# Fetching gathered rows and modulation weights ahead of their use, and keeping the first gates of a dense expert layer on chip

## The chip, the cores and the metric

The kernel runs on one core of a Trainium2 chip. TensorE (PE; its weight loads are PEld) multiplies matrices, VectorE (DVE) and ScalarE (ACT) do elementwise work, GpSimd (POOL) does some more of it and issues DMAs of its own, SyncE (SP) issues the other DMAs. Each engine takes its instructions strictly in order, and semaphores join them. The metric is the device time of one launch in microseconds (us). A measurement of this kernel can tell about 0.2% from no change.

## The reference, cut to what matters

Two networks run after one another on 256 tokens of 1024 columns in f32: a first block of two layers (gated feed-forward, then retention or latent attention with a memory, then feed-forward again), and a second block of two layers in which every norm is modulated by a vector computed from a conditioning input, and the feed-forward is a mixture of 16384 tiny experts:

```python
ml = (silu(c) @ mod_w[i] + mod_b[i]).reshape(bsz, 1, 6, d)      # modulation rows, latent
mc = (silu(c_ctx) @ mod_w[i] + mod_b[i]).reshape(6, d)          # the same for the context
xl = rmsnorm(hl, norm1_g[i]) * (1.0 + ml[:, :, 1]) + ml[:, :, 0]
...
def _peer_ffn(x, w_q, keys, u, v):       # 8 heads, 16 experts a head and token, of 128 x 128
    ...
    a = jnp.einsum('nd,nhkd->nhk', xt, u[eidx])
    w = gate * gelu(a)
    return jnp.einsum('nhk,nhkd->nd', w, v[eidx])
```

The second block has 256 context tokens beside the 256 latent ones. They pass through its first layer only.

## The kernel before

**Two streams.** The program is written by two generators that `run_streams` takes in turn. The main stream does the first block, then the even mixer, the expert layer `peer_dense(x, 0, 0)`, the odd mixer, `peer_dense(x, 1, 0)` and the final norm. The side stream does what the second block needs beforehand: modulation rows, the context's even mixer, its routing, and its expert layer. Each stream has a clock; what a generator yields is added to it (on the side divided by `s.rate`), the stream that is behind goes on, and the clock becomes the priority by which a scheduler orders the instructions of each engine. So a yielded number decides where an instruction stands. While a side ring of weight tiles is open, `dq` issues the side's DMAs on POOL, and otherwise on SP.

**Modulation.** Twelve slots of 1024 outputs, six a layer. A slot reads 4 MB of `modw` in eight tiles of 512 KB (`raw`, line 197, from a ring of `RN` = 3 tiles), and TensorE multiplies each tile in eight short matmuls (line 877). Two slots are done at the start, three beside the context's even mixer, the other seven (`mod1`) along with the gather. 96 tiles in all, each fetched where its matmuls are recorded.

**Context experts (gather).** For each of two tiles of 128 tokens, 128 rows of `u` are gathered by indirect DMA (`pg`, line 1586), one row a token at a time, and multiplied with the tokens by a DVE dot (line 306); then 128 rows of `v` are gathered and added up (line 1604). 512 gathers in all, into a ring of `GR` = 6 tiles. The odd mixer waits for the last of it (`hc1`).

**Latent experts (peer_dense).** All 16384 experts are multiplied densely, as 64 pairs of 256. `up` multiplies the tokens with `u` of a pair and keeps the result in `A`; `down` multiplies `A` with the gates of the pair (line 1686), splits the product into a high part `Wh` and a low part `Wl` (lines 259, 260), splits the weights of `v` likewise (`wh`, `wl`, lines 248, 255) and does three matmuls for each product (`mm3`, lines 357 to 359). Between the two, `spread_gates` turns the routing into dense gates in 16 blocks of 16 tokens: three DVE operations (`OJ`, `OI`, `OM`), 32 matmuls (line 1637), copies into a stage `Gst`, and a DMA of each block to DRAM (`Gd`). `down` reads them back by four pairs (`Gq`). `A0N` ups come before the spread, one a block follows until `AR` tiles of `A` are full, and the rest alternate with `down`. The first `NU` ups are single f32 products (line 404), the others are split into three.

Of the kernel before, what the change touches and what calls it, by code (L numbers as in the profile page):

```python
# [19 lines left out]
D = 1024  # L20
# [146 lines left out]
class Kern:  # L167
# [681 lines left out]
            yield from s.out_proj(x, mix, d["wo1"], g3)  # L849


    def modulation(s, l, side, slots):


        nc, d = s.nc, s.d
        qs = [(slice(32 * j, 32 * j + 32), slice(256 * j, 256 * j + 256)) for j in range(4)]
        with s.pool("mod", side) as pl:
            c = pl.tile([128, 8, 32], F32, name=s.nm("cT"))
            nc.vector.memset(c, 0.0)
            cr = pl.tile([128, 8, 2], F32, name=s.nm("cR"))  # L860
            s.dq(cr, d["cvecT"])
            nc.scalar.activation(c[:, :, 0:2], cr, AF.Silu)
            one = pl.tile([128, 32], F32, name=s.nm("one"))
            nc.vector.memset(one, 1.0)
            for a in slots:
                dr = s.dramp.tile([2, D], F32, name=s.nm("modd"))
                bias = pl.tile([128, 256], F32, name=s.nm("modb"), tag="modb")
                s.dq(bias[0:128:32], d[f"modb{l}"][0, a * D:(a + 1) * D].rearrange("(j n) -> j n", j=4))
                if a in (1, 4):
                    g = pl.tile([128, 256], F32, name=s.nm("modg"), tag="modg")  # L870
                    s.dq(g[0:128:32], d["n12r"][2 * l + a // 4].rearrange("(j n) -> j n", j=4))
                pb = s.bank("c")
                for k0 in range(0, 8, 2):
                    raw = s.load(d[f"modw{l}"][:, (a * 8 + k0) * D:(a * 8 + k0 + 2) * D])
                    for k in range(2):
                        for ps, ns in qs:
                            nc.tensor.matmul(pb[ps, :256], c[:, k0 + k], raw(k * D + ns.start, k * D + ns.stop),  # L877
                                             start=(k0 + k == 0), stop=False)
                    yield 3.0
                for ps, ns in qs:  # L880
                    nc.tensor.matmul(pb[ps, :256], one[ps.start:ps.start + 1], bias[ps.start:ps.start + 1], start=False, stop=True)
                o = pl.tile([128, 256], F32, name=s.nm("modo"), tag="modo")
                if a in (1, 4):
                    pg = s.bank("c")
                    for ps, ns in qs:
                        nc.tensor.matmul(pg[ps, :256], one[ps.start:ps.start + 1], g[ps.start:ps.start + 1], start=True, stop=True)
                    nc.vector.tensor_scalar(o, pb[:, :256], 1.0, None, op0=OP.add)
                    nc.vector.tensor_tensor(o, o, pg[:, :256], op=OP.mult)
                else:
                    nc.vector.tensor_copy(o, pb[:, :256])  # L890
                for v in range(2):
                    s.dq(dr[v].rearrange("(j n) -> j n", j=4), o[v:128:32])
                    s.mod[l, v, a] = dr[v:v + 1]
# [330 lines left out]
    def even(s, ep, x, l, v, C, kind, tk, side):  # L1224
# [4 lines left out]
        with s.pool("evo", side) as po:  # L1229
# [41 lines left out]
            with s.pool("eva", side) as pl:  # L1271
                if lat:
                    ks = ("acc", "w", "c")
                    yield from s.mlstm(pl, E, C, R, mix, ks)
                    yield from s.diff_attn(pl, E, C, R, mix, ks)
                else:
                    yield from s.taking_turns(s.mlstm_ctx(pl, E, R, mix, "c"), s.diff_attn_ctx(pl, E, R, mix, "c"),
                                              s.modulation(0, side, [2, 4, 3]))
            with s.pool("evp", side) as pl:
                xT = s.xt_tiles(None if lat else pl)  # L1280
                g = s.modrow(l, v, 2, pool=pl, tag="gate")
# [296 lines left out]
    def gather(s, hc, l, v, side, also):  # L1578

        nc, d = s.nc, s.d  # L1580
        xmd, eidx, gates = s.picks
        with s.pool("pgg", side) as op:
            for t in range(2):
                def gath(tab, k):
                    gt = op.tile([128, D], F32, tag="pgt", name=s.nm("pg"), bufs=s.gring)
                    nc.gpsimd.indirect_dma_start(out=gt, out_offset=None, in_=d[tab],  # L1586
                                                 in_offset=bass.IndirectOffsetOnAxis(ap=eidx[t][:, k:k + 1], axis=0))
                    return gt
                xm = op.tile([128, D], F32, tag="pxy", name=s.nm("pxm"))
                s.dq(xm, xmd[t])  # L1590
                A = op.tile([128, 128], F32, tag="pA", name=s.nm("pA"))
                for k in range(128):
                    s.pin(s.dot(gath("u0", k), xm, A[:, k:k + 1]))
                    if k % 2:
                        yield s.gcost + s.along(also)
                nc.scalar.activation(A, A, AF.Gelu)
                nc.vector.tensor_tensor(A, A, gates[t], op=OP.mult)
                y = op.tile([128, D], F32, tag="pxy", name=s.nm("py"))
                for k in range(128):
                    gt, wk = gath("v0", k), A[:, k:k + 1]  # L1600
                    if k == 0:
                        s.pin(nc.vector.tensor_scalar(y, gt, wk, None, op0=OP.mult))
                    else:
                        s.pin(nc.vector.scalar_tensor_tensor(y, gt, wk, y, op0=OP.mult, op1=OP.add))  # L1604
                    if k % 2:
                        yield s.gcost + s.along(also)
                g = s.modrow(l, v, 5, pool=op, tag="pgt", bufs=s.gring)
                x = op.tile([128, D], F32, tag="pgt", name=s.nm("px"), bufs=s.gring)
                s.dq(x, hc[t])
                nc.vector.tensor_tensor(y, y, g, op=OP.mult)  # L1610
                nc.vector.tensor_tensor(x, x, y, op=OP.add)
                s.dq(s.hc1[t], x)
                yield 0


    def spread_gates(s, Gd, IJ, gg, io, step):


        nc = s.nc
# [1 line left out]
        for b in range(256 // TB):  # L1621
# [11 lines left out]
            for t0 in range(0, TB, 4):  # L1633
                pb = s.bank("c")
                for t in range(4):
                    for k in range(2):
                        nc.tensor.matmul(pb[:, t * 128:(t + 1) * 128], M[:, k, :, t0 + t], OJ[:, (t0 + t) // 2, :, t % 2],  # L1637
                                         start=(k == 0), stop=(k == 1))
                nc.scalar.activation(st[:, :, t0:t0 + 4], pb.rearrange("p (t j) -> p j t", t=4), AF.Copy, scale=2.0 ** -15)
            s.dq(Gd[b], st.rearrange("p j t -> p (j t)"))  # L1640
            yield from step()

    def peer_dense(s, x, l, v):
        nc, d = s.nc, s.d
        TB = 16
        NP = 64
        A0N, AR = ((8, 21), (18, 36))[l]
        NU = (AR, A0N)[l]
        ud, vd = d[f"ut{l}"], d[f"v{l}"].rearrange("(i j) n -> i j n", j=128)
        with s.pool("pd") as op:  # L1650
# [18 lines left out]
                As[q] = op.tile([128, 2, 256], F32, tag="A", name=s.nm("A"), bufs=AR)  # L1669
                nc.scalar.activation(As[q].rearrange("p a b -> p (a b)"), pb, AF.Gelu)  # L1670

            Gq = {}

            def gates(q):

                if q < NP:
                    Gq[q] = sp.tile([128, 16, 8, TB], F32, tag="Gq", name=s.nm("Gq"), bufs=2)
                    s.dq(Gq[q].rearrange("p b j t -> p b (j t)"),
                         Gd[:, :, q * 2 * TB:(q + 4) * 2 * TB].rearrange("b p n -> p b n"))

            def down(q):
                raw = s.load(vd[:, 2 * q:2 * q + 2])
                w = As.pop(q)
                g = Gq[q // 4 * 4][:, :, q % 4 * 2:q % 4 * 2 + 2].rearrange("p b j t -> p j b t")
                wv = w.rearrange("p j (b t) -> p j b t", b=16)
                nc.vector.tensor_tensor(wv, wv, g, op=OP.mult)
                wh = sp.tile([128, 2, 256], F32R, tag="Wh", name=s.nm("Wh"), bufs=2)
# [31 lines left out]
            with s.pool("psp") as s.spp:  # L1719
                s.share = SH[l][1]  # L1720

                def step():
                    if nup[0] < AR:
                        up()
                        yield 5.2
                yield from s.spread_gates(Gd, IJ, gg, io, step)
            xfp.__exit__(None, None, None)
            with s.pool("ps") as sp:
                s.share = SH[l][2]
                gates(0)  # L1730
                for q in range(NP):
                    if q % 4 == 0:
                        gates(q + 4)
                    down(q)
                    if nup[0] < NP:
# [26 lines left out]
def build(ctx, tc, nc, d):  # L1762
# [43 lines left out]
    def side():  # L1806
        R = "right"
        yield from wait("start")
        with s.pool("pgo", R) as po:
            with s.pool("sraw", R) as rp:  # L1810
                with s.pool("shl", R) as hp:
                    s.rings["s"] = (rp, hp, RN, SB, 512, SL)
                    yield from s.modulation(0, R, [1, 0])
                    s.off = OFF["cev"]
                    yield from s.even(state["ep"], d["ctx"], 0, 1, None, "c", "c", R)
                    done.add("cev")
# [10 lines left out]
    def mod1():  # L1827
        with s.pool("sraw", "right") as rp:
            s.rings["s"] = (rp, None, RN, SB, 512, SL)
            yield from s.modulation(0, "right", [5])  # L1830
            yield from s.modulation(1, "right", [1, 0, 2, 4, 3, 5])
            del s.rings["s"]

    run_streams(s, nc, main(), side())
# [1 line left out]

WB = 2
SL = 2
RN = 3
FS = (1, 1)  # L1840
FN = 2
A0 = (1, 4)
# [2 lines left out]
DS = (1, 4)  # L1845
OFF = dict(mod1=0, cev=0, croute=0, pick=200, gather=200)
GR = 6
NR, NH, NL = (5, 3, 3)
CC = 6
RS = (0, 1)  # L1850
# [53 lines left out]
```

## Time and profile before

| | us |
|---|---|
| median of 3 runs | 3926.42 (3920.73, 3926.42, 3926.73) |
| the profiled execution, its own time | 3922.85 |
| its span | 3921.1 |
| PE busy | 3450.3 (88%) |
| DVE busy | 2809.8 (72%) |
| ACT busy | 1554.8 (40%) |
| POOL busy | 1484.0 (38%) |

The span is what the trace covers, so 1.75 us of the execution's own time lie around it. That time is 0.1% under the median. Starts in the trace count from the start of the span. The stages follow one another: modulation of two slots to 60 us, the first block to 1605, the even mixer to 1860, the first expert layer to 2860 (its spread from 2050 to 2181), the odd mixer to 3050, the second expert layer to 3905.

### The profile page before, as it was taken

To read this page: it belongs to the slowest core of one execution; us is meant where nothing else is said; L and a number is where in the kernel's file an instruction comes from. 1 tells how busy PE (TensorE), PEld (TensorE's weight loads), DVE (VectorE), ACT (ScalarE), POOL (GpSimd) and SP (SyncE) were. 2 spreads that over 40 slices of the span, in tenths; PEclk is the share of its full clock that TensorE was granted. 3 is DMA by queue.
4 is the path that set the end of the run, shared out by engine and by line. 5 is a ranking of instruction groups with operands and counts; after the bars stand their busy time and mean duration, and the time that the engine had idled before them with its cause. 6 is when DMAs were issued, how large, how long until landed. Compare 5 with 4: busy or idle time off the path is not lost.

```text
span 3921.1 us, 54952 instructions
## 1 busy us (share of the span) xinstructions
PE 3450.3 (88%) x20528; PEld 2940.2 (75%) x20528; DVE 2809.8 (72%) x5097; ACT 1554.8 (40%) x2399; POOL 1484.0 (38%) x1002
## 2 busy tenths in 40 slices
PE   5998977889898889788798799999878999999998
PEld 3775876678786678666687688888666789899987
DVE  4565798877777577887798788889875629754444
ACT  3453433334343433433122344444345115444444
POOL 3223325455555345432225477777610000121221
PEclk9999998789898889877899899999989999999999
DMA  7446539878788468752779999999841457886664
GB/s 265 138 161 204 191 110 376 282 275 295 264 293 315 164 247 295 272 199 97 236 260 365 318 331 329 329 332 329 308 146 38 136 154 246 274 254 209 198 193 152
DMA packets 316539, 939.18 MB, mean 240 GB/s; under 512 B 30432, under 2 KB 99536, under 8 KB 312176
## 3 DMA queue, kind: packets, MB, share of 16 engines
q1 hardware_dynamic: 216912, 579.82, 44.1%
q0 software_dynamic: 99360, 355.86, 25.9%
q8 instruction: 161, 2.64, 0.3%
q14 instruction: 106, 0.87, 0.1%
HBM read 895.88 MB, written 39.68 MB: 239 GB/s over the span
## 4 chain that ended last, share of the span: by engine, by line
PE 48%; DVE 16%; issue 14%; DMA 10%; POOL 8%; ACT 3%; POOLq 0%; DVEq 0%; ACTq 0%; SPq 0%
PE ps L357 11%; PE ps L358 11%; PE ps L359 11%; PE ps L404 7%; POOL pg L1586 4%; POOL wl L255 4%; DVE wl L255 3%; DMA raw<-in_ffn 3%; DMA raw<-in_modw 3%; DVE pg L306 2%; DVE py L1604 2%; PE ps L313 2%; ACT wh L248 1%; PE ps L1637 1%; PE ps L877 1%
## 5 line engine op out<-in xcount | busy, mean ns | idle before, releaser
L248 ACT CAST wh<-raw 128x1024 fp32r<-128x1024 f32 (+3 forms) x921 | 912.0, 992 | 1044.2 <-PE ps L359 735.8
L255 DVE TENSOR_TENSOR wl<-raw,wh 128x1024 fp32r<-128x1024 f32 (+2 forms) x660 | 813.7, 1236 | 499.1 <-ACT wh L248 497.7
L255 POOL TENSOR_TENSOR wl<-raw,wh 128x1024 fp32r<-128x1024 f32 (+3 forms) x261 | 620.9, 2380 | 1365.8 <-ACT wh L248 1257.5
L357 PE MATMUL ps<-xh,wl 128*128 128x256 f32 x2960 | 858.0, 290 | 60.3 <-POOL wl L255 32.4
L358 PE MATMUL ps<-xl,wh 128*128 128x256 f32 x2960 | 847.5, 286 | 0.0
L359 PE MATMUL ps<-xh,wh 128*128 128x256 f32 x2960 | 846.3, 286 | 0.0
L357 PEld LDWEIGHTS ps<-xh,wl 128*128 128x128 f32 x2960 | 576.2, 195 | 92.9 <-POOL wl L255 42.5
L358 PEld LDWEIGHTS ps<-xl,wh 128*128 128x128 f32 x2960 | 576.6, 195 | 5.4 <-issue 0.7
L359 PEld LDWEIGHTS ps<-xh,wh 128*128 128x128 f32 x2960 | 576.1, 195 | 1.2 <-issue 1.0
L1586 POOL DMA_INDIRECT pg<-in_u,eidx x256 | 364.8, 1425 | 438.8 <-DVE pg L306 252.2
L1586 POOL DMA_INDIRECT pg<-in_v,eidx x256 | 373.9, 1461 | 315.8 <-DVE py L1604 190.7
L358 PE MATMUL ps<-wl,Wh 128*128 128x512 f32 x1024 | 409.3, 400 | 26.8 <-DVE wl L255 15.3
L357 PE MATMUL ps<-wh,Wl 128*128 128x512 f32 x1024 | 404.6, 395 | 20.6 <-DVE Wl L260 20.6
L1604 DVE SCALAR_TENSOR_TENSOR py<-pg,pA,py 128x1024 f32<-128x1024 f32 x254 | 411.0, 1618 | 4.8 <-DMA pg<-in_v,eidx 1.5
L359 PE MATMUL ps<-wh,Wh 128*128 128x512 f32 x1024 | 402.6, 393 | 0.0
L404 PE MATMUL ps<-xf,raw 128*128 128x256 f32 x1760 | 397.0, 385 | 2.3 <-ACT xf L332 2.3
L404 PEld LDWEIGHTS ps<-xf,raw 128*128 128x128 f32 x1760 | 336.8, 194 | 48.4 <-ACT xf L332 3.1
L306 DVE SCALAR_TENSOR_TENSOR pg<-pg,pxm 128x1024 f32<-128x1024 f32 x256 | 329.7, 1311 | 9.7 <-DMA pg<-in_u,eidx 6.2
L358 PE MATMUL ps<-wl,xh 128*128 128x512 f32 (+4 forms) x656 | 255.2, 389 | 23.2 <-POOL wl L255 13.7
L357 PE MATMUL ps<-wh,xl 128*128 128x512 f32 (+4 forms) x656 | 250.0, 387 | 7.5 <-ACT wh L248 5.3
L358 PEld LDWEIGHTS ps<-wl,Wh 128*128 128x128 f32 x1024 | 195.0, 190 | 81.2 <-DVE wl L255 25.7
L359 PE MATMUL ps<-wh,xh 128*128 128x512 f32 (+4 forms) x656 | 250.5, 382 | 0.0
(479 smaller groups left out, 4769.8 us busy)
## 6 DMA issues: line engine op xcount, KB each, us to landing
raw<-in_ffn SPq DMA_DIRECT2D x264, 512.0 KB
raw<-in_ut SPq DMA_DIRECT2D x256, 512.0 KB
raw<-in_v SPq DMA_DIRECT2D x256, 512.0 KB
raw<-in_modw POOLq DMA_DIRECT2D x96, 512.0 KB
Gd<-Gst SPq DMA_DIRECT2D x32, 1024.0 KB
Gq<-Gd SPq DMA_DIRECT2D x32, 1024.0 KB
raw<-in_wq SPq DMA_DIRECT2D x32, 512.0 KB
raw<-in_evin POOLq DMA_DIRECT2D x24, 512.0 KB
```

What stands on the lines that cost most here:

```text
L248: nc.scalar.copy(hi, src)
L255: eng.tensor_tensor(lo, src, hi.bitcast(F32), op=OP.subtract)
L306: return s.nc.vector.scalar_tensor_tensor(a, a, 1.0, b, op0=OP.mult, op1=OP.mult, accum_out=out)
L313: s.nc.tensor.transpose(dst, src, s.ident[:src.shape[0], :src.shape[0]])
L357: mm(out, a[1], b[0], start=start, stop=False)
L358: mm(out, a[0], b[1], start=False, stop=False)
L359: mm(out, a[0], b[0], start=False, stop=stop)
L404: s.nc.tensor.matmul(out, src[:, k * 128:(k + 1) * 128], xf[:, k], start=(k == 0), stop=(k == 7))
L877: nc.tensor.matmul(pb[ps, :256], c[:, k0 + k], raw(k * D + ns.start, k * D + ns.stop), start=(k0 + k == 0), stop=False)
L1586: nc.gpsimd.indirect_dma_start(out=gt, out_offset=None, in_=d[tab], in_offset=bass.IndirectOffsetOnAxis(ap=eidx[t][:, k:k + 1], axis=0))
L1604: s.pin(nc.vector.scalar_tensor_tensor(y, gt, wk, y, op0=OP.mult, op1=OP.add))
L1637: nc.tensor.matmul(pb[:, t * 128:(t + 1) * 128], M[:, k, :, t0 + t], OJ[:, (t0 + t) // 2, :, t % 2], start=(k == 0), stop=(k == 1))
```

## The change

Three parts. **Modulation:** one tile of 512 KB is loaded for each k-block, and fetched `MP` = 2 tiles ahead, across slots too; the ring gets a fourth tile; the cost that is yielded becomes 8, 8 and 3 for the three calls (3 in all of them before) with one more yield at the start; the two calls of `mod1` become one; the tile `modo` is dropped, and the result overwrites `bias`. **Gather:** rows are fetched `GL` = 4 ahead, across `u`, `v` and the token tiles, in the same ring of six. **Gates:** the gates of the first two pairs are also copied on ACT from the stage into a tile `G0` that stays on chip (16 copies a layer), `Gq` begins with pair 2, and `AR` falls by 2 in both layers. In layer 0 `NU` is `AR`, so two of its ups become split ones and move from the spread to `down`.

```diff
-                for k0 in range(0, 8, 2):
-                    raw = s.load(d[f"modw{l}"][:, (a * 8 + k0) * D:(a * 8 + k0 + 2) * D])
-                    ...
-                    yield 3.0
+            units = [(l, a, k) for l, a in slots for k in range(8)]
+            def fetch(i):
+                if i < len(units):
+                    l, a, k = units[i]
+                    raws[units[i]] = s.load(d[f"modw{l}"][:, (a * 8 + k) * D:(a * 8 + k + 1) * D])
+            for i in range(MP):
+                fetch(i)
+            yield cost
...
+                for k in range(8):
+                    fetch(units.index((l, a, k)) + MP)
+                    raw = raws.pop((l, a, k))
+                    for ps, ns in qs:
+                        nc.tensor.matmul(pb[ps, :256], c[:, k], raw(ns.start, ns.stop), start=(k == 0), stop=False)
+                    if k % 2:
+                        yield cost
...
-                o = pl.tile([128, 256], F32, name=s.nm("modo"), tag="modo")
+                o = bias
...
+            def rows(t, tab):
+                for k in range(128):
+                    i = seq.index((t, tab, k))
+                    fetch(i + GL)
+                    yield k, got.pop(i)
...
+            nc.scalar.copy(G0[:, b], st[:, 0:G0.shape[2]])
             s.dq(Gd[b], st.rearrange("p j t -> p (j t)"))
...
-        A0N, AR = ((8, 21), (18, 36))[l]
+        A0N, AR = ((8, 19), (18, 34))[l]
...
+            G0 = op.tile([128, 16, 4, TB], F32, name=s.nm("G0"))
+            Gq = {0: (G0, 0), 1: (G0, 2)}
...
-                gates(0)
+                gates(2)
                 for q in range(NP):
-                    if q % 4 == 0:
+                    if q % 4 == 2:
                         gates(q + 4)
...
-            yield from s.modulation(0, "right", [5])
-            yield from s.modulation(1, "right", [1, 0, 2, 4, 3, 5])
+            yield from s.modulation("right", [(0, 5)] + [(1, a) for a in (1, 0, 2, 4, 3, 5)], MC[2])
...
-RN = 3
+RN = 4
+MP = 2
+MC = (8.0, 8.0, 3.0)
+GL = 4
```

On DVE, where the first layer's `down` begins, this stood before: the last block's `OM`, then the first products `A` with gates of the first `Gq`, the low parts `Wl` of pairs 0 and 1, further products, and the low part `wl` of a `v` tile of pair 1.

```order
L1631 TENSOR_TENSOR OM_19319<-OI_19317,gg_17193 128x4096
L255 TENSOR_TENSOR wl_19498<-raw_19487,wh_19496 128x1024
L1686 TENSOR_TENSOR A_18012<-A_18012,Gq_19367 128x512
L1686 TENSOR_TENSOR A_18041<-A_18041,Gq_19367 128x512
L1686 TENSOR_TENSOR A_18070<-A_18070,Gq_19367 128x512
L260 TENSOR_TENSOR Wl_19377<-A_18012,Wh_19376 128x512
L260 TENSOR_TENSOR Wl_19493<-A_18041,Wh_19492 128x512
L1686 TENSOR_TENSOR A_18099<-A_18099,Gq_19367 128x512
```

And this is there after the change, where line 1686 has become 1715:

```order
L1655 TENSOR_TENSOR OM_19244<-OI_19242,gg_17154 128x4096
L1715 TENSOR_TENSOR A_17980<-A_17980,G_17160 128x512
L1715 TENSOR_TENSOR A_18003<-A_18003,G_17160 128x512
L260 TENSOR_TENSOR Wl_19301<-A_17980,Wh_19300 128x512
L260 TENSOR_TENSOR Wl_19417<-A_18003,Wh_19416 128x512
L1715 TENSOR_TENSOR A_18032<-A_18032,Gq_19293 128x512
L1715 TENSOR_TENSOR A_18061<-A_18061,Gq_19293 128x512
L1715 TENSOR_TENSOR A_18090<-A_18090,Gq_19293 128x512
L1715 TENSOR_TENSOR A_18119<-A_18119,Gq_19293 128x512
L255 TENSOR_TENSOR wl_19426<-raw_19413,wh_19424 128x1024
```

The products and low parts of pairs 0 and 1 now need `G0` alone (`G_17160`), and the first instruction that needs a `Gq` has moved behind them, with `wl_19426` of pair 1 behind it.

On POOL, at the end of retention, this stood before: `modw` loads of `mod1`, gathers `pg` and low parts `wl` for the main stream.

```order
L197 DMA raw_8162<-in_modw 128x1024
L197 DMA raw_8164<-in_modw 128x1024
L197 DMA raw_8448<-in_modw 128x1024
L1586 DMA pg_9939<-in_u,eidx_2630 128x1024
L197 DMA raw_8450<-in_modw 128x1024
L197 DMA raw_8654<-in_modw 128x1024
L197 DMA raw_8656<-in_modw 128x1024
L197 DMA raw_8954<-in_modw 128x1024
L255 TENSOR_TENSOR wl_9719<-raw_9686,wh_9717 128x1024
```

And there is this on POOL after the change, at the same place:

```order
L197 DMA raw_8018<-in_modw 128x1024
L255 TENSOR_TENSOR wl_7359<-raw_7352,wh_7357 128x1024
L197 DMA raw_8024<-in_modw 128x1024
L197 DMA modd_7142<-modb_7143 4x256 x2
L197 DMA raw_8399<-in_modw 128x1024
L197 DMA raw_8405<-in_modw 128x1024
L197 DMA modb_8396<-in_modb 4x256
L197 DMA raw_8605<-in_modw 128x1024
L197 DMA raw_8611<-in_modw 128x1024
L197 DMA raw_8891<-in_modw 128x1024
L197 DMA raw_8897<-in_modw 128x1024
L197 DMA raw_9177<-in_modw 128x1024
```

Eight more loads now stand behind one another there, with two low parts (`wl_7387`, `wl_7545`) and the next gathers behind the last of them.

## Rows read from the trace of the kernel before

**Rows 1.** The page's first part: busy time, share, instructions of each engine.
```profile
PE 3450.3 (88%) x20528; PEld 2940.2 (75%) x20528; DVE 2809.8 (72%) x5097; ACT 1554.8 (40%) x2399; POOL 1484.0 (38%) x1002
```
**Rows 2.** Waits of the span: who waited for what, us in total, times, longest.
```profile
POOL pg L1586 <- DVE py L1604: 191.5, 88, 23.7
PE ps L877 <- DMA raw<-in_modw: 127.3, 40, 19.5
POOL raw L197 <- PE ps L877: 118.8, 41, 12.9
```
**Rows 3.** Timeline of PE at modw tiles: start, us, [idle before, releaser].
```profile
602.28 1.03 PE L877 MATMUL ps<-raw,cT 128*32 128x256 f32 x2 [19.48 <-DMA raw<-in_modw]
604.66 0.69 PE L313 MATMUL ps<-cst_base,xn 128*128 128x128 f32 x2 [1.35 <-DVE xn L338]
678.78 0.66 PE L877 MATMUL ps<-raw,cT 128*32 128x256 f32 x4 [5.07 <-DMA raw<-in_modw]
752.97 1.03 PE L877 MATMUL ps<-raw,cT 128*32 128x256 f32 x2 [10.39 <-DMA raw<-in_modw]
802.57 1.06 PE L877 MATMUL ps<-raw,cT 128*32 128x256 f32 x5 [11.25 <-DMA raw<-in_modw]
1030.81 1.08 PE L877 MATMUL ps<-raw,cT 128*32 128x256 f32 x8 [13.71 <-DMA raw<-in_modw]
1258.27 1.08 PE L877 MATMUL ps<-raw,cT 128*32 128x256 f32 x8 [11.02 <-DMA raw<-in_modw]
1298.94 0.65 PE L877 MATMUL ps<-raw,cT 128*32 128x256 f32 x4 [5.60 <-DMA raw<-in_modw]
```
**Rows 4.** Windows: us, busy us (instructions) by engine, granted clock, DMA share, GB/s.
```profile
20.00:40.00 20.00, 8.57 (x64) 1.60 (x64) 10.09 (x45) 7.84 (x23) 5.17 (x10) 1.00 1.00 375
340.00:360.00 20.00, 9.46 (x77) 3.42 (x78) 3.19 (x5) 3.44 (x6) 6.18 (x12) 0.74 0.76 237
730.00:750.00 20.00, 11.86 (x58) 4.49 (x56) 17.18 (x52) 3.99 (x13) 10.88 (x12) 0.50 0.82 286
```
**Rows 5.** Timeline of DVE behind the tile of 1258 us.
```profile
1260.42 0.42 DVE L887 TENSOR_SCALAR modo<-ps 128x256 f32<-128x256 f32 x1 [6.20 <-PE ps L881]
```
**Rows 6.** Timeline where the first layer's spread ends.
```profile
2180.84 0.33 SPq L197 DMA_DIRECT2D Gd<-Gst  x1
2186.02 2.15 SPq L197 DMA_DIRECT2D Gq<-Gd  x2
2192.18 1.90 DVE L1686 TENSOR_TENSOR A<-A,Gq 128x512 f32<-128x512 f32 x3 [12.47 <-DMA Gq<-Gd]
2194.74 0.80 PE L357 MATMUL ps<-wh,Wl 128*128 128x512 f32 x1 [14.55 <-DVE Wl L260]
```
**Rows 7.** Windows of the expert layers, columns as in rows 4.
```profile
2100.00:2140.00 40.00, 39.55 (x279) 35.34 (x277) 39.51 (x42) 12.31 (x22) 25.24 (x14) 0.99 0.99 380
2730.00:2820.00 90.00, 75.83 (x304) 56.35 (x303) 89.54 (x65) 33.03 (x38) 67.63 (x42) 0.98 0.94 345
3430.00:3820.00 390.00, 390.00 (x2319) 348.73 (x2319) 184.50 (x188) 182.72 (x210) 85.00 (x35) 1.00 0.69 213
```
**Rows 8.** Groups by line: busy, mean ns of one, idle before and its releasers.
```profile
L1604 DVE SCALAR_TENSOR_TENSOR py<-pg,pA,py 128x1024 f32<-128x1024 f32 x254 | 411.0, 1618 | 4.8 <-DMA pg<-in_v,eidx 1.5
L1631 DVE TENSOR_TENSOR OM<-OI,gg 128x4096 f16<-128x4096 f16 x32 | 73.2, 2286 | 12.0 <-PE ps L1637 11.9
L1625 DVE TENSOR_TENSOR OJ<-io,IJ 128x2048 f16<-128x2048 f16 x32 | 67.7, 2115 | 0.0
L1629 DVE TENSOR_TENSOR OI<-io,IJ 128x2048 f16<-128x2048 f16 x32 | 38.8, 1212 | 0.0
```
**Rows 9.** Timeline where the second layer's spread has ended.
```profile
3383.59 3.70 DVE L1686 TENSOR_TENSOR A<-A,Gq 128x512 f32<-128x512 f32 x3 [6.13 <-DMA Gq<-Gd]
3385.59 0.58 PE L357 MATMUL ps<-xh,wl 128*128 128x256 f32 x1 [3.61 <-POOL wl L255]
3387.95 0.29 PEld L357 LDWEIGHTS ps<-wh,Wl 128*128 128x128 f32 x1 [0.36 <-DVE Wl L260]
```

More of the change, by code (lines that the diff above doesn't have):

```diff
@@ L849, in mla, with modulation @@
             yield from s.out_proj(x, mix, d["wo1"], g3)
-    def modulation(s, l, side, slots):
+    def modulation(s, side, slots, cost):
         nc, d = s.nc, s.d
@@ L864, in modulation @@
             nc.vector.memset(one, 1.0)
-            for a in slots:
+            units = [(l, a, k) for l, a in slots for k in range(8)]
+            raws = {}
+            def fetch(i):
[5 more added lines that the diff above has]
+            yield cost
+            for l, a in slots:
                 dr = s.dramp.tile([2, D], F32, name=s.nm("modd"))
@@ L872, in modulation @@
                 pb = s.bank("c")
-                for k0 in range(0, 8, 2):
-                    raw = s.load(d[f"modw{l}"][:, (a * 8 + k0) * D:(a * 8 + k0 + 2) * D])
[L875 to L878, printed above, removed]
-                    yield 3.0
+                for k in range(8):
[5 more added lines that the diff above has]
+                        yield cost
                 for ps, ns in qs:
                     nc.tensor.matmul(pb[ps, :256], one[ps.start:ps.start + 1], bias[ps.start:ps.start + 1], start=False, stop=True)
-                o = pl.tile([128, 256], F32, name=s.nm("modo"), tag="modo")
+                o = bias
                 if a in (1, 4):
@@ L1277, in even @@
                     yield from s.taking_turns(s.mlstm_ctx(pl, E, R, mix, "c"), s.diff_attn_ctx(pl, E, R, mix, "c"),
-                                              s.modulation(0, side, [2, 4, 3]))
+                                              s.modulation(side, [(0, 2), (0, 4), (0, 3)], MC[1]))
             with s.pool("evp", side) as pl:
@@ L1581, in gather, with fetch @@
         xmd, eidx, gates = s.picks
+        seq = [(t, tab, k) for t in range(2) for tab in ("u0", "v0") for k in range(128)]
+        got = {}
         with s.pool("pgg", side) as op:
-            for t in range(2):
[L1584 to L1588, printed above, removed]
+            def fetch(i):
+                if i < len(seq):
+                    t, tab, k = seq[i]
+                    got[i] = op.tile([128, D], F32, tag="pgt", name=s.nm("pg"), bufs=s.gring)
+                    nc.gpsimd.indirect_dma_start(out=got[i], out_offset=None, in_=d[tab],
+                                                 in_offset=bass.IndirectOffsetOnAxis(ap=eidx[t][:, k:k + 1], axis=0))
+            def rows(t, tab):
[3 more added lines that the diff above has]
+                    yield k, got.pop(i)
+            for i in range(GL):
+                fetch(i)
+            for t in range(2):
                 xm = op.tile([128, D], F32, tag="pxy", name=s.nm("pxm"))
@@ L1591, in gather @@
                 A = op.tile([128, 128], F32, tag="pA", name=s.nm("pA"))
-                for k in range(128):
-                    s.pin(s.dot(gath("u0", k), xm, A[:, k:k + 1]))
+                for k, gt in rows(t, "u0"):
+                    s.pin(s.dot(gt, xm, A[:, k:k + 1]))
                     if k % 2:
@@ L1598, in gather @@
                 y = op.tile([128, D], F32, tag="pxy", name=s.nm("py"))
-                for k in range(128):
-                    gt, wk = gath("v0", k), A[:, k:k + 1]
+                for k, gt in rows(t, "v0"):
+                    wk = A[:, k:k + 1]
                     if k == 0:
@@ L1613, in gather, with spread_gates @@
                 yield 0
-    def spread_gates(s, Gd, IJ, gg, io, step):
+    def spread_gates(s, Gd, G0, IJ, gg, io, step):
         nc = s.nc
@@ L1670, in up @@
                 nc.scalar.activation(As[q].rearrange("p a b -> p (a b)"), pb, AF.Gelu)
-            Gq = {}
+            G0 = op.tile([128, 16, 4, TB], F32, name=s.nm("G0"))
+            Gq = {0: (G0, 0), 1: (G0, 2)}
             def gates(q):
                 if q < NP:
-                    Gq[q] = sp.tile([128, 16, 8, TB], F32, tag="Gq", name=s.nm("Gq"), bufs=2)
-                    s.dq(Gq[q].rearrange("p b j t -> p b (j t)"),
-                         Gd[:, :, q * 2 * TB:(q + 4) * 2 * TB].rearrange("b p n -> p b n"))
+                    n = min(4, NP - q)
+                    g = sp.tile([128, 16, 8, TB], F32, tag="Gq", name=s.nm("Gq"), bufs=2)[:, :, :2 * n]
+                    s.dq(g.rearrange("p b j t -> p b (j t)"),
+                         Gd[:, :, q * 2 * TB:(q + n) * 2 * TB].rearrange("b p n -> p b n"))
+                    Gq.update({q + i: (g, 2 * i) for i in range(n)})
             def down(q):
@@ L1683, in down @@
                 w = As.pop(q)
-                g = Gq[q // 4 * 4][:, :, q % 4 * 2:q % 4 * 2 + 2].rearrange("p b j t -> p j b t")
+                g, j0 = Gq.pop(q)
+                g = g[:, :, j0:j0 + 2].rearrange("p b j t -> p j b t")
                 wv = w.rearrange("p j (b t) -> p j b t", b=16)
@@ L1725, in step @@
                         yield 5.2
-                yield from s.spread_gates(Gd, IJ, gg, io, step)
+                yield from s.spread_gates(Gd, G0, IJ, gg, io, step)
             xfp.__exit__(None, None, None)
@@ L1812, in side @@
                     s.rings["s"] = (rp, hp, RN, SB, 512, SL)
-                    yield from s.modulation(0, R, [1, 0])
+                    yield from s.modulation(R, [(0, 1), (0, 0)], MC[0])
                     s.off = OFF["cev"]
```

## The prediction

> **What bounds the kernel now.** I begin with the busy times [rows 1]. PE works 3450.3 us of a span of 3921.1 us and is therefore idle for 470.8 us, 12%; no other engine comes near it over the whole span. So the first question is what ends PE's idle time, and the second is which of it lies where nothing else could have run. The list of waits answers the first [rows 2]: PE's matmuls of modulation weights wait 127.3 us, 40 times, for the DMA of their tile, the largest wait of PE for a transfer. The reverse stands in the same list: POOL, which issues these loads, waits 118.8 us until a matmul has freed a tile of the ring of three. The timeline at those matmuls answers the second [rows 3], and it has to be read one wait at a time, since the work that follows is often a norm that isn't ready either. Last come the windows [rows 4, 7]: a stall is worth what it says only where PE is full before and after it. In the second expert layer's `down` PE is busy 390.00 us of 390.00, so what is saved ahead of it reaches the end. In the first one's tail DVE is busy 89.54 of 90 us and PE 75.83, so there DVE decides.
>
> **The change part by part, modulation.** 96 tiles stay 96 tiles, and 768 matmuls stay. What is new is a fourth tile and an issue two tiles ahead, so that a load no longer waits for the matmul before it.
>
> At the start PE works 8.57 us of 20 between 20 and 40 us, but the DMA engines have a share of 1.00 at 375 GB/s [rows 4]: earlier issue only queues there. I take −3 us, between 0 and −8. The Trainium skill (DMA: Bandwidth & Descriptors, Bandwidth) gives about 358 GB/s as what HBM yields to one core; the row is already above it, and by the page this term would be nothing, 3 us less gain.
>
> From 320 to 360 us the share is 0.76 and PE works 9.46 of 20 us in the second half [rows 4], a tile at a time as loads land. One more tile in flight can't give all of the 10.5 us back, since each load still takes its time; I take −7, between 0 and −10.5.
>
> Then come the single stalls [rows 3]. At 602.28 PE idles 19.48 us, but the transposes behind it could only start at 604.66, with the norm: nothing to win. The change even puts the first load of this batch behind ten gathers on POOL instead of six, and its matmuls behind those transposes, ahead of retention's projections; +3, between 0 and +6. At 678.78 and 752.97 PE idles 5.07 and 10.39 us inside retention, and around the second the clock stands at 0.50 for 20 us [rows 4]. More than half should go: −9, between 0 and −20. At 802.57, 11.25 us lie in the change from retention to the feed-forward, where the norm is also on its way; I take nothing, at best −6. At 1030.81 it is 13.71 us in the same kind of place; −4, between 0 and −8. At 1258.27 PE idles 11.02 us, and this wait does more: a DVE operation of the modulation waits 6.20 us for the group's last matmul, until 1260.42 [rows 5], and the small operations of the norm stand behind it on DVE, which is in order. So the stall delays the norm that would otherwise hide it: −6, between 0 and −11. At 1298.94, 5.60 us with ready work behind: −5, between 0 and −5.6. Sum: −3−7+3−9−4−6−5 = −31, with the bounds adding up to +6 and −69; all ends together are unlikely, and I use −10 to −48.
>
> **The gather.** Fetching four ahead costs nothing and should win nothing by itself. The ring has six tiles as before, and DVE is idle ahead of the `v` rows for 1.5 us in all because of a gather [rows 8]; it is POOL that waits for DVE to free tiles, 191.5 us for the `v` rows alone [rows 2]. 0.
>
> **The gates, first layer.** The last block goes out to DRAM at 2180.84, its return is issued at 2186.02, the first product runs at 2192.18 and PE begins `down` at 2194.74 after 14.55 us of idling [rows 6]. With pairs 0 and 1 from `G0`, PE can start as soon as a copy on ACT, a product (1.90 us for three, 0.63 each) and two splits have passed, at about 2183.5. But on DVE the products of pairs 2 to 5 follow, which need the `Gq` of about 2192, and a weight split that pair 1 needs stands behind them. A pair is 24 matmuls of 512 columns, an up 48 of 256, as many columns; the full window has 2319 matmuls in 390 us, 32.2 steps of 72, so 12.1 us a step and 6.05 for either half [rows 7]. PE does pair 0 and half of pair 1, about 9 us at most, then waits until 2192.2 + 4 × 0.63 + 1.2 for the split, about 2196. It has then 1.5 pairs done where before it had 0.2: 1.3 × 6 = 7.8 us, and the low clock of a restart stays. I take −7, between 0 and −12.
>
> Two ups leave the spread. There PE and DVE are both full, 39.55 and 39.51 of 40 us, and 279 matmuls at 64 a block make 4.36 blocks, 9.2 us each [rows 7]. A block without an up still costs DVE 2.29 + 2.12 + 1.21 = 5.6 us [rows 8], so each of the two wins at least 3.6 us and, if DVE has other work to give PE, up to 7: −9, between −7 and −14. The same two ups come back as split ones in `down`, 6.05 us each on PE, +12, and their four weight splits take DVE, POOL or ACT time. The shorter spread also lets fewer gather operations pass DVE ahead of `down`. The order puts four more `v` rows into its last third, 4 × 1.62 us [rows 8] in the stretch where DVE is full: +6, between 0 and +10. The 32 copies to `G0` go on ACT, which is busy 40% of the span [rows 1]; they are hidden by the matmuls of the next block, and if that cover were missing, 16 of about 0.3 us would cost 5 us a layer. First layer: −7−9+12+6 = +2, between −14 and +15.
>
> **The gates, second layer.** DVE waits 6.13 us for `Gq` until 3383.59, and behind it stand weight splits; PE idles 3.61 us at 3385.59 and starts pair 0 at 3387.95 [rows 9]. In the new order the splits of the last up stand ahead of the first `Gq` wait. I take −6, between −3 and −10, and it reaches the end, since PE is full behind it.
>
> **Sum.** −31 + 0 + 2 − 6 = −35. The profiled execution took 3922.85 us, so 3888; against the median of 3926.42, which is 3.6 us longer, the forecast is 3889.
>
> **The rivals.** *Hidden anyway.* The stalls of modulation lie beside norms (as at 602.28 and 802.57), and the norm is what ends last: then only the inner ones, 678.78, 1298.94 and a part of 320 to 360, give anything, some 12 us, the first layer takes 2 back, and the second gives its 6: 3926 − 16 = about 3910. For it speaks that the norm is named within 3 us of the first stall; against it that DVE is held by a modulation group at 1260.42 [rows 5].
>
> *Slower, because POOL is in order.* After the change ten loads of weights stand behind one another on POOL at the end of retention. With four tiles, the fifth waits for a matmul that stands at the norm, and the main stream's splits and the gathers stand behind it. POOL already waits 118.8 us for such matmuls [rows 2]. If a split that PE needs is held until the norm is past, PE loses about a stall of 10 to 13 us at each of the three transitions (802, 1030, 1258), +35 in all, and the gain of −14 inside retention and at 1298.94 is what remains, with the −6 of the second layer: 3926 + 35 − 20 = about 3941. The point that decides is whether a split that PE needs within some 10 us stands behind the fifth load. Against it: DVE takes most of the splits, and gathers are ahead of need.
>
> *Larger, by the clock.* Around 752.97 the clock is 0.50, 1.2 instead of 2.4 GHz, for 20 us in which PE works 11.86 [rows 4]. If without the stalls it stayed at 2.4, half of that work time, 6 us, returns there, and as much near 345 us, 1030 and 1258: −24 on top, about 3865. The Trainium skill (TensorE: Matmul & The Clock Gate, HAM oscillation) says this too: waits for transfers between short bursts of matmuls let the clock fall, and each burst restarts cold. The rows at 340 and 730 agree, 0.74 and 0.50.
>
> *No effect.* With the matmuls recorded at other places, new waits eat the old ones, and the time stays within 0.2%, 7.9 us, which is about what a measurement of this kernel can tell from no change: 3922.
>
> **How the numbers follow.** My forecast of around 3889 (3872 to 3905) has 0.46, hidden anyway 0.16, larger 0.15, no effect 0.10, slower 0.13. Faster by more than 0.2% are the first three, 0.77; same 0.10; slower 0.13. For 8 in 10 the range reaches from 3857, past the larger case's middle, to 3930, which leaves out most of the slower case and the tail below.
>
> **What would show it.** PE's wait for modulation tiles falls from 127.3 to under 70 us, with shares still below 60 us at the start. The matmuls of 1258 no longer hold DVE for 6 us, and the granted clock between 730 and 770 rises above 0.8. The first `down` pair of layer 0 starts within 4 us of the last block's copy, then PE waits at pair 1 for a split behind a `Gq` wait. The spread of layer 0 gets about 9 us shorter and its `down` as much longer. In the second layer the 3.61 us go. The prediction is wrong if POOL's splits show up as PE's releaser at the norms with 10 us each, or if the gather ends so late that the odd mixer waits for it, or if PE idles as long at those norms for DVE as it did for the tiles.

## The result and the profile after

The changed kernel takes 3899.68 us (median of 6 runs, 3889.61 to 3902.65), before took 3929.44 beside it (6 runs): a ratio of 0.9916, 95% interval 0.9894 to 0.9938. The same kernel measured again (e5 below) gave 3904.77 us and 0.9953 (0.9937 to 0.9969; 9 runs against 27). By these ratios the change wins 33 us the first time and 18 the second; the forecast was 35. The profiled execution took 3902.65 us, its span 3899.7, 21.4 less than that of before.

The first part of the page after, to be read against [rows 1]:

```profile
PE 3444.3 (88%) x20560; PEld 2939.3 (75%) x20560; DVE 2800.3 (72%) x5086; ACT 1564.8 (40%) x2432; POOL 1507.2 (39%) x1014
```

PE is busy 6.0 us less than before, and 455.4 us of idling are left of 470.8. PE's waits after, over the whole span (us in total, times, longest), answer to [rows 2]:

```profile
PE ps L888 <- DMA raw<-in_modw: 64.8, 32, 6.9
...
PE ps L313 <- DVE sm L285: 32.0, 2, 23.0
```

PE's wait for modulation tiles has halved, from 127.3 us to 64.8, the forecast's first sign. But the span is shorter by only a third of these 62 us: PE waits for a norm instead, and the last row has grown from 11.0 us to 32.0. The timeline of PE in the changes of stage (start, us, [idle before, releaser]) shows where, against [rows 3]:

```profile
586.60 1.94 PE L313 MATMUL ps<-cst_base,xn 128*128 128x128 f32 x8 [23.01 <-DVE sm L285]
...
1006.81 1.08 PE L897 MATMUL ps<-modg,one 1*32 1x256 f32 x8 [5.98 <-DVE sm L276]
1014.45 1.08 PE L888 MATMUL ps<-raw,cT 128*32 128x256 f32 x8 [6.56 <-DMA raw<-in_modw]
```

Ahead of retention PE idled 19.48 us for a tile, then 1.35 for the norm; now it idles 23.01 us for the norm alone. The tile was hidden there, as the prediction had it for that place, but it turns out so elsewhere too. How far the two kernels are apart at the same piece of work tells more than any wait. I take six marks in each trace: the silu of the first feed-forward's last tile (A), the first copy to `Gst` of layer 0's spread (B; 2034.5 us before, so this spread begins there and not at 2050), the first transposes of the odd mixer's keys (`otw`, C), the first copy of layer 1's spread (D), the split of `A` for its ninth pair (E), and the end. Between them pass, in us of the profiled executions:

```
kernel                              to A    A-B    B-C    C-D    D-E   E-end
before                             567.8 1466.7  853.7  363.9  209.9  459.1
after                              548.9 1467.4  852.5  360.3  211.6  459.1
e1 modulation alone                543.8 1467.4  858.4  364.3  209.4  459.1
e2 gather alone                    562.9 1470.1  862.7  363.7  209.5  459.1
e3 gates alone                     568.0 1464.8  863.8  358.9  211.6  459.1
e4 whole, ring of three            564.9 1470.9  856.2  359.8  215.5  459.2
e5 whole again                     542.2 1467.1  859.0  363.7  210.8  459.1
e6 modulation and gather           545.2 1470.3  858.5  364.0  209.6  459.1
e7 modulation and gates            550.1 1474.8  849.3  359.8  215.2  459.1
e8 whole, no lead                  546.6 1464.5  856.3  359.7  211.6  459.2
e9 fourth tile for context only    546.4 1474.2  857.1  359.8  211.7  459.1
e10 fourth tile for mod1 only      571.6 1461.9  855.4  363.7  215.1  459.2
e11 gates in layer 0 only          547.0 1466.6  856.3  360.0  209.7  459.1
e12 modulation three, rest four    562.3 1479.2  859.9  359.7  211.6  459.1
```

Of the 21.4 us that the changed kernel is ahead at the end, 18.9 lie ahead of A, in the first 550 us. Between A and B, where the prediction had two thirds of modulation's gain, nothing is won. The windows say the same, first to A, before and after, then from A to B (columns as in [rows 4]):

```profile
0.00:567.80 567.80, 473.53 (x2923) 378.24 (x2923) 347.88 (x1022) 243.81 (x420) 167.86 (x196) 0.94 0.54 181
0.00:548.90 548.90, 468.65 (x2923) 376.66 (x2923) 331.11 (x1013) 243.58 (x421) 180.01 (x205) 0.95 0.55 187
567.80:2034.50 1466.70, 1232.23 (x7230) 1040.99 (x7230) 1142.63 (x2350) 539.44 (x927) 643.72 (x463) 0.88 0.73 255
548.90:2016.30 1467.40, 1233.69 (x7231) 1044.04 (x7231) 1128.96 (x2336) 537.59 (x924) 636.96 (x456) 0.88 0.72 253
```

To A PE runs the same 2923 matmuls and idles 80.3 us in place of 94.3; from A to B it idles 233.7 us in place of 234.5. What shortens C to D in eight of the ten profiles with the gates changed in layer 0 (358.9 to 360.3 us, against 363.7 to 364.3 in all others) no run shows. Single executions scatter: the two profiles of the changed kernel (after and e5) differ by 6.7 us to A and 6.5 us from B to C, so only what is larger, or the same in many kernels, is read from this table.

### The profile page after: what moved, and what is told of

Same layout as the page of the kernel before. It is cut to its first block, busy times and chain, and to the rows that moved or that the text cites. A ratio compares the mean times of both kernels' runs of the same rounds, so it can differ in the third digit from the quotient of the medians.

```text
span 3899.7 us, 55086 instructions
## 1 busy us (share of the span) xinstructions
PE 3444.3 (88%) x20560; PEld 2939.3 (75%) x20560; DVE 2800.3 (72%) x5086; ACT 1564.8 (40%) x2432; POOL 1507.2 (39%) x1014
## 4 chain that ended last, share of the span: by engine, by line
PE 34%; issue 10%; DVE 9%; POOL 7%; DMA 5%; ACT 2%; POOLq 0%; SPq 0%; DVEq 0%; ACTq 0%
PE ps L357 8%; PE ps L358 8%; PE ps L359 7%; PE ps L404 6%; POOL pg L1600 4%; POOL wl L255 3%; PE ps L313 1%; DMA raw<-in_ffn 1%; DVE py L1628 1%; DVE wl L255 1%; DVE pg L306 1%; PE ps L1661 1%; DMA raw<-in_ut 1%; PE ps L1112 1%; ACT wh L248 1%
## 5 line engine op out<-in xcount | busy, mean ns | idle before, releaser
L255 POOL TENSOR_TENSOR wl<-raw,wh 128x1024 fp32r<-128x1024 f32 (+2 forms) x274 | 641.5, 2342 | 1342.4 <-ACT wh L248 1239.2
L255 DVE TENSOR_TENSOR wl<-raw,wh 128x1024 fp32r<-128x1024 f32 (+3 forms) x651 | 799.7, 1233 | 404.5 <-ACT wh L248 403.7
L357 PE MATMUL ps<-xh,wl 128*128 128x256 f32 x2992 | 868.0, 290 | 69.2 <-POOL wl L255 38.9
L358 PE MATMUL ps<-xl,wh 128*128 128x256 f32 x2992 | 857.2, 287 | 0.0
L359 PE MATMUL ps<-xh,wh 128*128 128x256 f32 x2992 | 856.2, 286 | 0.0
L404 PE MATMUL ps<-xf,raw 128*128 128x256 f32 x1696 | 382.8, 386 | 2.3 <-ACT xf L332 2.3
L404 PEld LDWEIGHTS ps<-xf,raw 128*128 128x128 f32 x1696 | 325.3, 194 | 47.2 <-ACT xf L332 3.1
L306 DVE SCALAR_TENSOR_TENSOR pg<-pg,pxm 128x1024 f32<-128x1024 f32 x256 | 341.8, 1360 | 11.6 <-DMA pg<-in_u,eidx 11.4
```

Source lines behind the costliest of these rows:

```text
L255: eng.tensor_tensor(lo, src, hi.bitcast(F32), op=OP.subtract)
L306: return s.nc.vector.scalar_tensor_tensor(a, a, 1.0, b, op0=OP.mult, op1=OP.mult, accum_out=out)
L357: mm(out, a[1], b[0], start=start, stop=False)
L358: mm(out, a[0], b[1], start=False, stop=False)
L359: mm(out, a[0], b[0], start=False, stop=stop)
L404: s.nc.tensor.matmul(out, src[:, k * 128:(k + 1) * 128], xf[:, k], start=(k == 0), stop=(k == 7))
```

## The experiments

All ratios are to the kernel before, run beside, from 7 to 12 runs of a version and 17 to 35 of before.

**e1 to e3: one part at a time.** Edits: only the hunks of `modulation`, `RN`, `MP` and `MC`; only those of `gather` and `GL`; only those of `spread_gates` and `peer_dense`.

> Only the modulation part of the change (fetch two tiles ahead, ring of four, yields of 8, 8 and 3, one joined call); gather and gates as before. Theory A, from the two traces: this part is the whole of what reaches the end, because at the first block of Gates (Gst) of layer 0 the changed kernel was 18 us ahead and at its end 21 us. It expects 18 to 30 us less than before, a ratio of 0.992 to 0.9955. Rival B: the parts work together (the gather's place decides how long DVE and POOL hold the norms), and alone the modulation gives under 10 us, a ratio above 0.997.

> Only the gather's fetch four rows ahead; the rest as before. Theory A: the ring of six and DVE set the gather's pace, not the moment of issue, so the time stays within 4 us of before (0.999 to 1.001). Rival B: the gathers stand ahead of the modulation loads on POOL, and the time changes by more than 8 us (below 0.998 or above 1.002).

> Only the gates of the first two pairs on chip, with A rings of 19 and 34; the rest as before. Theory A: in layer 0 a spread 9 us shorter and a stall 7 us shorter are paid back by two split ups of 6 us and some waits in the down phase, in layer 1 the earlier start comes back as a later wait for Gq; in sum 4 us less to 4 us more (0.999 to 1.001). Rival B, the prediction: layer 1 keeps its 6 us, and the ratio is about 0.998.

Measured: modulation 0.9983 (0.9968 to 0.9998; 12 runs), gather 1.0011 (0.9998 to 1.0024), gates 1.0011 (0.9995 to 1.0027). The gather and the gates win nothing, as theory A has it for both. Modulation's ratio lies in B's band; its profiled execution, the shortest of its twelve, is 18.6 us ahead at the end and 24.0 at A.

**e4: the whole with three tiles.**

```diff
-RN = 4
+RN = 3
```

> The whole change, but with the side ring of 3 tiles of before in place of 4. Theory A: it is the fourth tile that lets a load run while two wait for their matmuls, so most of the modulation's gain goes: 10 to 20 us over the changed kernel, a ratio to before of 0.995 to 0.998. Rival B: what counts is where loads and matmuls are recorded (two tiles ahead, other yields); then three tiles do as well within 5 us, a ratio of 0.991 to 0.993.

Measured: 1.0007 (0.9991 to 1.0022). Without the fourth tile nothing is left at all, more than theory A asked for. At A it is 2.9 us ahead of before.

**e5 to e8: the whole again, pairs of parts, and no lead.** e6 is e1 with e2's edit, e7 is e1 with e3's. e8:

```diff
-MP = 2
+MP = 0
```

> The whole change once more, beside the next three. Theory A: the first measurement holds (0.9916, interval 0.9894 to 0.9938), so the three parts are worth more together, 33 us, than alone (7 less, 4 more and 4 more). Rival B: the executions of this kernel scatter by 0.3% up and down, six of them fell low, and the whole is really 0.995 to 0.998.

> Modulation and gather changed, gates as before. Theory A: both issue on POOL and their matmuls and dots share the way through the norms, so they are what works together: a ratio of 0.991 to 0.995. Rival B: they add up as alone, 7 less and 4 more: 0.998 to 1.000.

> Modulation and gates changed, gather as before. Theory A: the gates come behind the modulation and have nothing to do with it, so this stays at the modulation alone, 0.997 to 0.9995. Rival B: it is the gates that gain when the modulation is out of the way, 0.991 to 0.995.

> The whole change with a lead of 0 tiles in place of 2: each modulation tile is recorded as loaded right ahead of its matmuls; ring of four, yields and the rest as changed. Theory A: the lead in the program is what lets a load go out ahead of other work on POOL, and without it 10 to 25 us are lost (ratio to before 0.995 to 1.000). Rival B: the ring of four sets the lead alone, and the time stays within 5 us of the whole.

Measured: whole 0.9953 (0.9937 to 0.9969), modulation and gather 0.9960 (0.9946 to 0.9974), modulation and gates 0.9965 (0.9948 to 0.9982), no lead 0.9957 (0.9944 to 0.9970). For e5 theory B holds: in the first measurement the changed kernel's median was 5.1 us lower than here and that of before 5.7 us higher. The four are the same within their intervals, and e1's overlaps with each of them; whether the other two parts add some us to modulation alone stays open. e8 is plain: theory B holds, the lead of two tiles in the program is worth nothing where the ring has four. No run has the ring of four without the rest of the modulation part (other yields, one tile a load, one joined call). So e4 shows that the fourth tile is needed, and none shows that it is enough.

**e9 and e10: where the fourth tile works.** The side ring is made twice, for the context's stage (to about 490 us) and for `mod1`. e9, and e10 the other way round:

```diff
-            s.rings["s"] = (rp, None, RN, SB, 512, SL)
+            s.rings["s"] = (rp, None, 3, SB, 512, SL)
```

> The whole change, with the ring of four tiles only while the first five modulation slots and the context's even mixer run, and three tiles again for the seven slots along the gather. Theory A, from the stages of nine profiles: the gain arises before 550 us, and the loads in the changes around 600 to 1310 us lie in the shade of norms, so this keeps all of it: 0.993 to 0.9965, with the end of the first feed-forward's silu (its last one) 18 to 26 us earlier than before. Rival B, the prediction: the stalls in retention and at the later norms carry two thirds of the gain, so 0.998 to 1.000.

> The reverse: three tiles at the start and beside the context, four for the seven slots along the gather. Theory A: nothing is left, 0.999 to 1.001, as for the ring of three throughout. Rival B: 0.994 to 0.997.

Measured: context only 0.9968 (0.9952 to 0.9984), 21.4 us ahead at A; `mod1` only 1.0011 (0.9996 to 1.0027), 3.8 us behind at A. Theory A's numbers came in both, within 0.0003 in the ratios. e9's interval alone would just allow rival B (0.998); the 21.4 us at mark A don't, and e10 leaves B nothing. In e10 PE waits less for modulation tiles over the span than in e9, and it is the slower one. The row of each in the list of waits, first e9, then e10:

```profile
PE ps L888 <- DMA raw<-in_modw: 90.9, 30, 14.9
```
```profile
PE ps L888 <- DMA raw<-in_modw: 79.5, 38, 8.4
```

**e11: gates in layer 0 only.**

```diff
-            G0 = op.tile([128, 16, 4, TB], F32, name=s.nm("G0"))
-            Gq = {0: (G0, 0), 1: (G0, 2)}
+            G0, Gq, NG = None, {}, (2, 0)[l]
+            if NG:
+                G0 = op.tile([128, 16, 4, TB], F32, name=s.nm("G0"))
+                Gq = {0: (G0, 0), 1: (G0, 2)}
...
```

> The whole change, but layer 1 reads all its gates back from DRAM as before (its A ring 36 again). Theory A: in layer 1 the gates on chip are given back by the next wait for a Gq; from the first block of its spread to the ninth pair the profiles show 209.4 to 209.9 us without them and 210.8 to 215.5 us with, so this falls to 209 to 210 and the time is 1 to 5 us below the whole (0.993 to 0.9955). Rival B, the prediction: without them 6 us are lost, and the stretch is above 214 us.

Measured: 0.9953 (0.9936 to 0.9970), D to E 209.7 us. Theory A's stretch is there, 2 us better than with the gates; the whole time is the same as the changed kernel's. This is as good as any version here, and with less in it.

**e12: whose tile is it?** In the context's stage, modulation's loads turn over in three of the four tiles, and the other loads in all four.

```diff
+            if ring is s.rings.get("s") and ring[1] is not None:
+                s.nload += not s.inmod
+                tag, bufs = ("raw", 3) if s.inmod or s.nload % 4 else ("raw4", 1)
...
```

> The whole change, and the context's ring of four is told apart by its user: tiles of modulation weights turn over in three of the four, those of the context's mixer and router (evin, evout, wq) in all four. Theory A: the fourth tile gains at the context's output projection and router queries, whose loads follow the modulation in the same ring (in the profiles with three tiles the eight evout loads are issued over 28 to 31 us, with four over 18); then at least two thirds of the 17 to 25 us by the end of the first feed-forward's silu are kept, and the ratio is 0.994 to 0.998. Rival B, the prediction's reason: it gains by having a further modulation tile in flight, then little is left, under 8 us, and the ratio is 0.998 to 1.001.

Measured: 1.0000 (0.9984 to 1.0016), 5.5 us ahead at A. Rival B's numbers came, but its reason isn't shown by them: the edit held back both users. The seven later `evout` loads had to wait for tiles that modulation still held, and were issued as late as with three (up to 369.63 us). Nor does PE's wait for modulation tiles tell winners from losers: up to 550 us it is 30.0 us in e12 and 31.0 in e8, which wins. The wait of ACT's cast for `evout` between 330 and 400 us does, in the list of waits of before, e4, e12, and then the changed kernel:

```profile
ACT wh L248 <- DMA raw<-in_evout: 11.1, 2, 10.0
```
```profile
ACT wh L248 <- DMA raw<-in_evout: 10.5, 1, 10.5
```
```profile
ACT wh L253 <- DMA raw<-in_evout: 10.5, 1, 10.5
```
```profile
ACT wh L248 <- DMA raw<-in_evout: 3.1, 1, 3.1
```

The six profiles in which modulation has three tiles there wait 9.0 to 11.1 us, the eight in which it has four 3.0 to 3.2. PE's idle time up to A divides them the same way: 91.4 to 95.9 us against 75.5 to 80.8.

## Why the prediction was right, and where its steps failed

The time lies in the range and the sign was right; that the size fits the first measurement so well is luck. The repeat's 3904.77 us lies at the very end of the range, and its 18 us are half of the 35. Two errors took back a part of each other: 9 us more than forecast were won ahead of A, and 22 fewer between A and B. (One slip in the sum: 3926.42 − 35 is 3891, not 3889.)

**The start and the context's stage: two terms about right, one left out.** The terms −3 (start) and −7 (320 to 360 us) make −10. The last matmul of the two slots at the start begins at 59.0 us before and 56.5 after, and PE's work from 340 to 360 us rises from 9.46 to 17.52 us. At the last modulation matmul of the context's stage (354.9 us before, 343.6 after) the kernel is 11.3 us ahead, about as forecast, and the reason given, one more tile in flight, fits: 10.3 to 14.1 us in the eight profiles in which modulation has four tiles there, 7.2 at most in the others. But to A it won 18.9 us, and 17.7 to 25.6 in those eight. What I left out is that the ring is shared. Behind the last modulation tiles stand the loads of the context's output projection (`evout`) in the same ring and on the same queue. POOL's timeline, first and last `evout` load, in the changed kernel:

```profile
340.52 0.53 POOL L197 DMA_DIRECT2D raw<-in_evout  x1 [0.71 <-PE ps L888]
...
359.03 0.55 POOL L197 DMA_DIRECT2D raw<-in_evout  x1 [0.87 <-issue]
```

And with three tiles (e4):

```profile
342.30 0.53 POOL L197 DMA_DIRECT2D raw<-in_evout  x1 [0.54 <-PE ps L888]
...
372.60 0.54 POOL L197 DMA_DIRECT2D raw<-in_evout  x1 [0.66 <-DVE wl L255]
```

The first is only 1.8 us apart, the last 13.6. Against before (last `evout` load at 379.41), the changed kernel's lead grows by 9.1 us between the last modulation matmul and the last `evout` load; in the eight profiles with four tiles this is 8.8 to 10.4 us, in the other five at most 5.2. With three tiles (e4) the kernel is 7.2 us ahead at the last modulation matmul and 6.8 at the last `evout` load, and only 2.9 are left at A. How much of the 11 us would reach A without the 9 no run separates: e12 held back both.

**The later stalls: the step that failed.** The terms +3, −9, 0, −4, −6 and −5 make −21 for 600 to 1310 us, with the reason that work stood ready behind the tile, or, at 1258, that the wait held up the norm on DVE. From A to B it was 0.7 us more. DVE's wait of 6.20 us [rows 5] did go, and nothing was won by it. e9, with three tiles in this part, still waits 90.9 us for modulation in all and wins as much as the range of the others; e10, with four there alone, wins nothing. So these stalls were in the shade of norms, as the rival *hidden anyway* said, and it was the right one for this half. Two things took the place of the tiles: PE waits for DVE's norms (23.01 us at 586.60, 5.98 at 1006.81), and inside the second and third feed-forward PE waits more for POOL's splits, as the *slower* rival had it, only smaller. Those waits of PE after, from 830 to 1235 us:

```profile
PE ps L357 <- POOL wl L255: 13.9, 10, 2.8
```

Before it was 6.0 us, between 850 and 1245.

**The clock: back near 345 us, at little gain.** The larger rival's condition came true there. The row of 340 to 370 us before, after and in e4:

```profile
340.00:370.00 30.00, 18.83 (x108) 9.59 (x109) 4.57 (x7) 6.13 (x11) 13.55 (x20) 0.77 0.67 203
```
```profile
340.00:370.00 30.00, 24.62 (x120) 16.50 (x117) 15.97 (x20) 9.58 (x16) 16.72 (x24) 0.94 0.80 264
```
```profile
340.00:370.00 30.00, 20.33 (x91) 12.95 (x84) 11.64 (x14) 6.15 (x11) 12.96 (x18) 0.77 0.68 216
```

The granted clock, a mean of stretches at 1.2 and at 2.4 GHz, is 0.94 to 1.00 here in the eight profiles with four tiles, and 0.77 to 0.83 in the other six. The Trainium skill (TensorE: Matmul & The Clock Gate, HAM oscillation) has it that waits for transfers between bursts of matmuls let the clock fall, and these rows agree. Inside retention it rose less than forecast: 0.51 from 730 to 770 us before, 0.63 from 712 to 752 after, about the same work 18 us earlier; from A to B as a whole it is 0.88 in both. The 6 us a place that this rival priced don't show: PE's busy time to A fell by 4.9 us, and by as much in e12 (468.73 us), which has 0.81 in that row and wins nothing.

**The gather: right.** Forecast 0; alone 1.0011, an interval that holds 1.

**Gates, first layer: right in its terms.** Compared with the first copy to `Gst` (18.2 us ahead), the first copy of the last block is 8.6 us further ahead (−9 forecast), and the cast `Wh` of pair 0 another 7.5 (−7). The timeline after, against [rows 6]:

```profile
2154.72 0.32 SPq L197 DMA_DIRECT2D Gd<-Gst  x1
...
2155.00 1.29 DVE L1715 TENSOR_TENSOR A<-A,G 128x512 f32<-128x512 f32 x2 [4.63 <-ACT G L1664]
2158.64 1.14 ACT L259 CAST Wh<-A 128x512 fp32r<-128x512 f32 x2 [3.68 <-DMA Gd<-Gst]
...
2160.04 0.80 PE L357 MATMUL ps<-wh,Wl 128*128 128x512 f32 x1 [5.98 <-DVE Wl L260]
```

DVE has the product at once, but the cast `Wh` waits 3.68 us for the last block's DMA, which must have left `Gst` before its place can be written. So PE starts 5.3 us behind the copy to `G0`, not within 4. Then it runs on: the forecast wait at pair 1 didn't come, since DVE's split followed at 2167.56 and POOL took the next at 2168.34. Between pairs 40 and 48 the lead falls from 35.1 to 21.9 us, 13 for the two split ups (12 forecast). The tail cost 2 to the last pair, not 6. B to C came out at −1.2 (+2 forecast), and from 4 us less to 10 more in the other versions.

**Gates, second layer: wrong in sign.** Counted from D, the cast `Wh` of pair 0 starts 9.8 us earlier, and yet D to E, up to the ninth pair, is 1.7 us longer. My step was that PE is full behind it, so that a gain must reach the end. But the earlier start only meets the next wait sooner. The timeline after, DVE and then PE, against [rows 9]:

```profile
3382.84 3.78 DVE L1715 TENSOR_TENSOR A<-A,Gq 128x512 f32<-128x512 f32 x3 [3.63 <-DMA Gq<-Gd]
```
```profile
3387.80 0.39 PE L357 MATMUL ps<-xh,wl 128*128 128x256 f32 x1 [3.77 <-DVE wl L255]
```

Products for the next pairs wait for their `Gq`, and the split that PE needs stands behind them on DVE; the same pair of waits comes again at 3410.13 and 3415.39 us (3.67 and 3.40 us). So the 3.61 us of [rows 9] didn't go. From D to E the nine profiles with gates on chip in layer 1 show 210.8 to 215.5 us, the five without them 209.4 to 209.9. The window of full PE that I leaned on begins at 3430 us, past these waits.

## What to carry to other kernels

A stall of PE is worth its length only if what stands behind it was ready: compare the two kernels at the same piece of work, not wait by wait, since 62 us of waits went here and 21 came off the span. When a ring or a queue is shared, a part of what a tile more gives can appear at the next user's loads, so follow the ring past the instruction that is named in the wait. An earlier start of a stage counts only as far as its next wait for the same resource; look one step behind the stall that goes.

## What the runs showed of the hardware that I had not expected

Executions of one kernel scatter by 0.3% up and down, and with the clock: in e8 twelve executions lie between 3894.86 and 3919.97 us with mean granted clocks from 0.929 to 0.937, the higher clock with the lower time (correlation −0.91, about 2.7 us for each 0.001). Which of the two is the cause isn't shown. Means over the runs of a version differ as well: 0.931 to 0.935 in the versions that win, 0.929 to 0.932 in those that don't and in before. The scatter is as much as most of the parts measured here: the ratio of one and the same kernel came out at 0.9916 from six runs of each side and at 0.9953 from nine and 27.
